# Two-layer hybrid mixing block: matmuls of a set recorded as one scheduled piece, and the first loads and small chains in another order

## The chip, the cores and the metric

The kernel runs on one core of one Trainium2 chip. The metric is the device time of one execution in microseconds (us); lower is better. The core has a matrix engine (TensorE, PE in the profile, with its weight loads as PEld), a vector engine (VectorE, DVE), an activation engine (ScalarE, ACT), a general engine (GpSimd, POOL) and SyncE (SP), which issues the loads and stores here. Matmuls write to the accumulation memory PSUM; all other tiles lie in the on-chip memory SBUF.

## The reference

Two layers of a block on 512 latent tokens and 256 context tokens of width 1024, all in fp32. Each layer makes six modulation vectors from the condition, mixes the tokens in four parallel groups, and ends with a squared-ReLU MLP:

```python
for layer in range(DEPTH):                      # DEPTH = 2
    sh1, sc1, g1, sh2, sc2, g2 = adaln(c, w_mod[layer], b_mod[layer])
    y_ctx, y_lat = mixing_sublayer(modulate(cx, csh1, csc1), modulate(x, sh1, sc1), ...)
    x = x + g1 * y_lat
    x = x + g2 * sq_relu_mlp(modulate(x, sh2, sc2), mlp_w1[layer], mlp_w2[layer])
    # the context cx likewise, in the first layer only
return rms_norm(x, final_g)
```

`adaln` is `silu(cond) @ w + b`, cut into six rows; `modulate` is `rms_norm(x) * (1 + scale) + shift`. `mixing_sublayer` projects the tokens by `w_in` (1024 x 2464) and splits the columns into a gated depthwise convolution of 31 taps, a latent attention (MLA), a grouped attention (GQA), and a chunked retention in two directions whose decay comes from `ret_decay`; the four results go through `w_out`.

## The kernel before

The kernel is written as a list of operations that are recorded, not issued. Each call on `V`, `S`, `G`, `T` or `D` (DVE, ACT, POOL, PE, and SP for loads) goes to `Plan.record`, which notes the operation with its inputs, outputs, an estimated duration and a priority, the place in the recording plus `plan.lag`. `Plan.schedule` then places all operations by a list scheduler: at every moment each engine takes the ready operation of the lowest priority that has room for its tiles. Some operations may go to DVE, ACT or POOL (`VS`, `VG`, `VSG`), and the planner picks the engine. Only then is everything issued, in that order; each engine runs its instructions in order. As all calls go through `issue`, they carry one line number in the profile, L646 before and L662 after.

Large matmuls are made from three fp32r products (`mm3`: high x low, high x high, low x high) with up to 512 columns. Other matmuls run in fp32; each is then two records in the trace. Three kinds of these fill only a part of the array's 128 columns and are meant to lie beside each other:

- `mod_rows` (line 792), a block of a modulation row: 4 matmuls of 32 columns each, one for every 128 rows of a half of the inner dimension, with 256 or 512 output columns. Their left side is `sf`, the silu of the condition.
- `Duo.finish` (line 1070), the output of an attention for a pair of heads: 12 matmuls (4 for context tokens) of 64 columns, two heads in turn, 256 output columns.
- The output of the retention (`s_ret`, line 1434): full-width matmuls with the states and then matmuls of 64 columns for two heads in turn, 128 or 256 output columns.

Before, each of these matmuls was an operation of its own to the planner, with a price for 64 columns or fewer that assumes the neighbour.

The order in which the parts are recorded is written out in the table `ORDER`, one string per layer: `um`, `ug` and `ur` are parts of the input projection, `mla`, `gqa`, `a`, `taps`, `gates`, `ln`, `rin`, `ret`, `read` steps of the four groups, `u` a step of an attention unit, and `todo:n` the n-th later modulation block of layer 0.

At the start the kernel loads the condition (`crow`), makes `sf`, then records the rotary tables `r64` and `r32`, the chain that makes the logarithm of the retention decay (`lgam` from `lz`, some 25 tiny DVE steps and two ACT steps), then the first modulation blocks (`mods(0)`, as `XO` is 0), and for the context pair (tokens 4 and 5) and the two pairs of x: load, sum of squares on ACT, reciprocal root on POOL, scaling, transposes, copies (`xt`, `norm_T`). After that `begin(q)` modulates a quarter of the inner dimension and `um` multiplies it by its quarter of `w_in`, four times (`late`).

## Time and profile before

| what | value |
|---|---|
| median of three runs | 1684.92 us (1681.69 to 1686.33) |
| the profiled execution | 1679.99 us |
| its span, first to last instruction | 1678.3 us |
| PE busy | 1630.6 us, 97% of the span |
| DVE busy | 1234.1 us, 74% |
| ACT busy | 569.9 us, 34% |
| POOL busy | 256.0 us, 15% |
| mean load rate | 98 GB/s |

Busy time is the time in which at least one instruction of the engine runs; matmuls are pipelined, so a busy PE is not a PE at its peak. What a run of matmuls costs is read from the start of its first to the start of what stands behind it. A wait is put down to the engine or load that ended last.

### The profile page before, as it was taken

How to read it: one execution, taken by the hardware profiler on the slowest of the kernel's cores; microseconds unless marked ns; L12 is line 12 of the kernel's file. 1: busy time of each engine (PE TensorE's matmuls, PEld its weight loads, DVE VectorE, ACT ScalarE, POOL GpSimd, SP SyncE). 2: the span in 40 equal slices, each digit the busy share in tenths (PEclk: the TensorE clock that was granted, in tenths of full speed). 3: DMA queues.
4: the chain of work that ended last, by engine and by line, in shares of the span. 5: the costliest groups of instructions: out<-in, count | busy, mean ns of one | idle time of the engine just before them, and what ended most of it. 6: DMA issues, size and time to landing. Idle time of an engine off the chain costs nothing. (4 is left out here: it accounts for less than half of the span.)

```text
span 1678.3 us, 22457 instructions
## 1 busy us (share of the span) xinstructions
PE 1630.6 (97%) x8603; PEld 1337.5 (80%) x8603; DVE 1234.1 (74%) x2093; ACT 569.9 (34%) x1008; POOL 256.0 (15%) x274
## 2 busy tenths in 40 slices
PE   6999999979999999999999999999989999999997
PEld 4888875657888888888888889788768888888886
DVE  5669956686876978767765667698888766666665
ACT  4431555474351111211211126345472512212212
POOL 2121102143010000010000013303032100000001
PEclk9999999999999999999999999999999999999999
DMA  8412126332322443534421212111125232333331
GB/s 298 135 51 58 51 79 181 102 114 88 98 79 88 127 141 96 164 112 126 151 63 51 74 51 86 46 53 33 53 76 169 83 101 91 98 100 94 95 100 51
DMA packets 138906, 164.03 MB, mean 98 GB/s; under 512 B 7466, under 2 KB 94106, under 8 KB 138800
## 3 DMA queue, kind: packets, MB, share of 16 engines
q1 hardware_dynamic: 138800, 162.61, 31.7%
q8 instruction: 67, 1.10, 0.3%
q14 instruction: 39, 0.32, 0.1%
HBM read 156.56 MB, written 2.10 MB: 95 GB/s over the span
## 5 line engine op out<-in xcount | busy, mean ns | idle before, releaser
L646 PE MATMUL b<-m,m 128*128 128x512 f32 (+5 forms) x6468 | 1316.5, 368 | 8.5 <-DVE m L646 5.8
L646 PEld LDWEIGHTS b<-m,m 128*128 128x128 f32 (+1 forms) x6468 | 1083.1, 185 | 221.8 <-DVE m L646 10.9
L646 DVE TENSOR_TENSOR m<-m,m 128x512 f32<-128x512 f32 (+5 forms) x510 | 457.8, 913 | 69.9 <-PE b L646 56.2
L646 ACT CAST m<-m 128x1024 fp32r<-128x1024 f32 (+3 forms) x219 | 197.4, 916 | 616.7 <-PE b L646 443.7
L646 DVE TENSOR_TENSOR m<-b,m 128x512 f32<-128x512 f32 (+9 forms) x309 | 183.1, 606 | 134.9 <-PE b L646 115.6
L646 POOL TENSOR_TENSOR m<-m,m 128x1024 fp32r<-128x1024 f32 (+5 forms) x67 | 130.3, 1949 | 821.0 <-ACT m L646 449.9
L646 PE MATMUL pp<-m,m 128*128 128x512 f32 (+8 forms) x876 | 180.7, 350 | 3.6 <-ACT m L646 1.9
L646 PEld LDWEIGHTS pp<-m,m 128*128 128x128 f32 (+2 forms) x876 | 134.1, 182 | 37.5 <-issue 11.4
L646 DVE TENSOR_TENSOR m<-m 128x512 f32<-128x512 f32 (+1 forms) x100 | 59.2, 592 | 95.1 <-ACT m L646 94.8
L646 PE MATMUL b<-ident,m 128*128 128x128 f32 (+3 forms) x740 | 109.1, 283 | 12.6 <-DVE m L646 9.1
L646 PEld LDWEIGHTS b<-ident,m 128*128 128x128 f32 (+3 forms) x740 | 86.5, 143 | 35.5 <-DVE m L646 12.1
L646 ACT ACTIVATE m<-b 128x512 f32<-128x512 f32 (+1 forms) x115 | 60.9, 532 | 140.6 <-PE b L646 136.3
L646 DVE SCALAR_TENSOR_TENSOR m<-m,sf,m 128x1024 f32<-128x1024 f32 x80 | 101.8, 1284 | 7.5 <-DMA m<-in_w_mod_dram 7.4
L646 DVE SCALAR_TENSOR_TENSOR m<-m,cvw,m 128x783 f32<-128x783 f32 (+1 forms) x120 | 102.0, 896 | 0.4
L646 ACT COPY m<-b 128x512 f32<-128x512 f32 (+4 forms) x109 | 57.2, 542 | 112.3 <-PE b L646 110.3
L646 DVE TENSOR_REDUCE ty<-pp 128x1 f32<-128x768 f32 (+1 forms) x70 | 62.9, 906 | 12.1 <-PE pp L646 10.8
L646 ACT ACTIVATE m<-pp,ty 128x768 f32<-128x768 f32 (+1 forms) x70 | 60.4, 865 | 31.4 <-DVE ty L646 22.1
L646 DVE CAST m<-m 128x512 fp32r<-128x512 f32 (+4 forms) x126 | 58.9, 471 | 7.5 <-PE b L646 2.6
L646 POOL TENSOR_TENSOR ty<-ty,mhalf 128x1 f32<-128x1 f32 (+4 forms) x47 | 56.3, 1202 | 3.1
L646 ACT ACTIVATE m<-m 128x1024 f32<-128x1024 f32 (+4 forms) x65 | 42.3, 654 | 38.0 <-DVE m L646 37.5
L646 DVE TENSOR_SCALAR m<-m,ty 128x512 f32<-128x512 f32 (+3 forms) x94 | 45.0, 512 | 11.6 <-POOL ty L646 10.9
L646 POOL TENSOR_SCALAR ty<-ty 128x2 f32<-128x2 f32 (+4 forms) x43 | 12.6, 292 | 229.4 <-ACT m L646 163.6
(109 smaller groups left out, 620.8 us busy)
## 6 DMA issues: line engine op xcount, KB each, us to landing
m<-in_mlp_w_dram SPq DMA_DIRECT2D x128, 512.0 KB
m<-in_w_mod_dram SPq DMA_DIRECT2D x96, 512.0 KB
m<-in_w_in_dram SPq DMA_DIRECT2D x32, 512.0 KB
m<-in_w_out_dram SPq DMA_DIRECT2D x16, 512.0 KB
m<-in_x_dram SPq DMA_DIRECT2D x8, 512.0 KB
m<-in_w_in_dram SPq DMA_DIRECT2D x8, 416.0 KB
m<-m SPq DMA_DIRECT2D x24, 96.0 KB
m<-in_ctx_dram SPq DMA_DIRECT2D x4, 512.0 KB
```

The costliest lines, as they stand in the source:

```text
L646: op.fn(*[f(a) for a in op.args], **{k: f(a) for k, a in op.kw.items()})
```

## The change

Four edits, and a new table:

- A class `_Tensor` adds `burst`: a list of matmuls is recorded as one operation, whose inputs and outputs are those of all. The planner places it as a whole, and issues its matmuls one behind the other. `mod_rows`, `Duo.finish` and the retention output use it. Its price is 94 ns plus the columns, in proportion to the share of the array.
- The start: the context pair is recorded ahead of the first modulation blocks (`XO = 1`), and the first quarter of the weights of `um` is loaded with them (`w0`). The rotary tables, the decay chain and `own` move from ahead of all this to behind `begin(0)`. A one-element Silu (`warm`) on ACT is recorded ahead of `srow`.
- The convolution's constants of layer 0 (`cdw`, `prm`) get a later priority, 400 places (`PL`).
- `ORDER` has new strings for both layers; all groups keep their steps.

```diff
-XO = 0
+PL = 400
+XO = 1
...
+class _Tensor(_Engine):
+    def burst(self, mms):
+
+        def go(mms):
+            for o, l, r, start, stop in mms:
+                self._r.matmul(self._p.bind(o), lhsT=self._p.bind(l), rhs=self._p.bind(r), start=start, stop=stop)
+
+        return self._p.record(self._n, self._r, go, (), {"mms": mms})
...
+        for o, l, r, _, _ in kw.get("mms", ()):
+            outs.append(o)
+            ins += [l, r]
...
+        if "mms" in kw:
+            return 94 + sum(4 * n(o) / 2.4 * l.ap[-1][1] / 128 for o, l, _, _, _ in kw["mms"])
...
             if ins[0].dtype == F32:
-                if ins[0].ap[-1][1] <= 64:
-                    return 4 * size / 2.4 * ins[0].ap[-1][1] / 128
                 return max(4 * size, 256) / 2.4 + 7
...
+    warm = cst([128, 1], "warm")
+    S.activation(out=warm, in_=mhalf[:, 0:1], func=AF.Silu)
     srow = cst([16, 128], "srow")
...
-            for k in range(4):
-                T.matmul(o[32 * k:32 * k + 32], lhsT=sf[:, k0 + k], rhs=rs[k // nk][:, k % nk], start=k0 == 0, stop=k0 > 0)
+            T.burst([(o[32 * k:32 * k + 32], sf[:, k0 + k], rs[k // nk][:, k % nk], k0 == 0, k0 > 0) for k in range(4)])
...
+        plan.lag = 0 if l else PL
         cdw = smt([31, 256], nm="cdw")
...
+        plan.lag = 0
...
-                ws = [load(0)]
+                ws = list(w0)
...
-                for j in range(n):
-                    for k in range(2):
-                        T.matmul(o[64 * k:64 * k + 64], lhsT=self.vst[k](self.kts[j]), rhs=self.pts[k][j // 2][:, j % 2],
-                                 start=j == 0, stop=j == n - 1)
+                T.burst([(o[64 * k:64 * k + 64], self.vst[k](self.kts[j]), self.pts[k][j // 2][:, j % 2], j == 0, j == n - 1)
+                         for j in range(n) for k in range(2)])
...
         if XO == k:
             mods(0)
+            w0.append(load_w(kview(w_in[0], 512, 928)[:, 0:2], 2, 416))
         xt.update({t: load_x(t) for t in pr})
```

In the retention output the calls of `T.matmul` become entries of a list `mms`, which `T.burst(mms)` records. One of the strings of `ORDER`, the end of layer 0, before and after:

```
"todo:5 taps:4 rin taps:1 u:1 ret u:1 taps ln:1 u:3 ln:1 u:1 read:1 u:2 ln u:3 read:1 u read "
"todo:4 todo:5 u:1 taps:7 rin u:1 ret u:2 taps u:2 ln u:3 read:1 u:2 read:1 u:1 read u "
```

**Where instructions move.** In an order row stand the line, the operation, output and inputs, the output's shape, and how many alike follow each other; `m`, `b` and `pp` are SBUF pages and PSUM banks.

PE in the mixing of layer 0, before: modulation sets (those with `sf`) between transposes and attention scores.

```order
L646 MATMUL b_3212<-m_5571,sf 32x512 x2
L646 MATMUL pp_5391<-ident,m_4637 128x128
L646 MATMUL pp_5390<-ident,m_4699 128x128 x2
L646 MATMUL pp_5390<-ident,m_4800 128x128
L646 MATMUL b_3212<-m_5581,sf 32x512 x2
L646 MATMUL pp_5390<-ident,m_4800 128x128
L646 MATMUL pp_5391<-m_5579,m_5623 128x256 x2
L646 MATMUL b_3213<-m_5579,m_5623 128x256 x2
L646 MATMUL b_3212<-m_5602,sf 32x512
L646 MATMUL pp_5687<-m_5242,m_5512 128x512
L646 MATMUL pp_5687<-m_5218,m_5512 128x512 x2
L646 MATMUL pp_5687<-m_5218,m_5512 128x256 x3
```

After, a place of the same stage:

```order
L662 MATMUL pp_5562<-m_5392,m_5346 128x512
L662 MATMUL pp_5562<-m_5369,m_5346 128x512 x2
L662 MATMUL pp_5562<-m_5369,m_5346 128x256 x3
L83 MATMUL b_3214<-m_5453,sf 32x512 x2
L83 MATMUL b_3214<-m_5508,sf 32x512 x2
L662 MATMUL b_3216<-ident,m_4117 128x128
L662 MATMUL b_3216<-ident,m_5413 128x128
```

The four matmuls of a set, cut into pieces of two or of one before, stand together now, under L83.

PE in the mixing of layer 1, before: the last pieces of an attention set (64x256) whose first matmul stands some 20 rows further up.

```order
L646 MATMUL pp_13590<-ident,m_13573 128x128
L646 MATMUL pp_13590<-ident,m_13596 128x128
L646 MATMUL b_3213<-m_13599,m_12085 64x256
L646 MATMUL pp_13663<-m_13037,m_13319 128x512
L646 MATMUL pp_13663<-m_13319 128x512
L646 MATMUL pp_13663<-m_13153,m_13319 128x256
L646 MATMUL pp_13663<-m_13319 128x256
L646 MATMUL b_3213<-m_13582,m_12085 64x256
L646 MATMUL b_3213<-m_13599,m_12085 64x256
L646 MATMUL b_3213<-m_13582,m_12146 64x256
L646 MATMUL b_3213<-m_13652,m_12146 64x256
```

After, a set of this stage, with the scores of the next unit ahead of it:

```order
L662 MATMUL pp_13334<-m_13181,m_13087 128x512
L662 MATMUL pp_13334<-m_13154,m_13087 128x512 x2
L662 MATMUL pp_13334<-m_13154,m_13087 128x256 x3
L662 MATMUL pp_13351<-m_13181,m_13087 128x512
L662 MATMUL pp_13351<-m_13154,m_13087 128x512 x2
L83 MATMUL b_3216<-m_12357,m_11877 64x256
L83 MATMUL b_3216<-m_13325,m_11877 64x256
```

The set of 12, of which the first two rows are shown, is no longer cut by scores.

ACT at the start, before: `g` is made from the end of the decay chain, and the rows with 128x1024 are the sums of squares of the context and of x.

```order
L646 ACT_TABLE_LOAD
L646 ACTIVATE srow<-crow 16x128
L646 ACTIVATE lz<-lgam 128x16
L646 ACT_TABLE_LOAD
L646 ACTIVATE lz<-lz 128x16
L646 ACTIVATE g_724<-lgc 128x2
L646 ACTIVATE g_2264<-lgc 128x2
L646 ACTIVATE m_3373,ty_3190<-m_3279 128x1024
L646 ACTIVATE m_3383,ty_3190<-m_3282 128x1024
```

After:

```order
L662 ACT_TABLE_LOAD
L662 ACTIVATE warm<-mhalf 128x1
L662 ACTIVATE srow<-crow 16x128
L662 ACTIVATE m_3282,ty_3191<-m_3231 128x1024
L662 ACTIVATE m_3296,ty_3191<-m_3239 128x1024
L662 COPY m_3328<-b_3215 128x512
L662 COPY m_3328<-b_3216 128x512
```

The steps of the decay chain no longer stand ahead of the squares; on SP the two loads of the context stand third and fourth, where they were twelfth and thirteenth.

## Rows read from the trace of the kernel before

**Rows 1.** Page, part 1: engine, busy us, share of the span, instructions.

```profile
PE 1630.6 (97%) x8603; PEld 1337.5 (80%) x8603; DVE 1234.1 (74%) x2093; ACT 569.9 (34%) x1008; POOL 256.0 (15%) x274
```

**Rows 2.** Stretches: length, busy PE PEld DVE ACT POOL, granted clock, load share, GB/s.

```profile
0.00:42.00 42.00, 26.32 (x168) 18.32 (x172) 24.27 (x85) 19.19 (x36) 9.54 (x40) 1.00 0.90 298
...
190.00:400.00 210.00, 199.37 (x1213) 137.48 (x1212) 152.37 (x314) 125.05 (x242) 52.86 (x61) 0.99 0.36 110
400.00:1030.00 630.00, 628.77 (x3234) 538.26 (x3232) 461.03 (x630) 150.01 (x248) 58.05 (x58) 1.00 0.33 101
1030.00:1330.00 300.00, 289.16 (x1708) 238.28 (x1707) 245.88 (x508) 146.62 (x268) 74.26 (x64) 1.00 0.25 73
```

**Rows 3.** Waits of PE, whole span: us in total, times, longest.

```profile
PE b L646 <- DVE m L646: 14.9, 15, 2.9
```

**Rows 4.** Order in time, PE, layer 0: start, us, what, records; modulation pieces.

```profile
270.12 1.05 PE L646 MATMUL b<-m,sf 128*32 128x512 f32 x4
271.10 0.66 PE L646 MATMUL pp<-ident,m 128*128 128x128 f32 x4
...
273.47 1.05 PE L646 MATMUL b<-m,sf 128*32 128x512 f32 x2
274.44 1.32 PE L646 MATMUL pp<-m,m 96*128 96x512 f32 x6
```

**Rows 5.** Order in time, PE, layer 1: an attention set in three pieces.

```profile
1220.86 0.65 PE L646 MATMUL b<-m,m 128*64 128x256 f32 x2
1221.43 0.30 PE L646 MATMUL pp<-ident,m 128*64 128x128 f32 x1
...
1224.56 0.63 PE L646 MATMUL b<-ident,m 128*128 128x128 f32 x4 [0.77 <-DVE m L646]
...
1226.88 0.65 PE L646 MATMUL b<-m,m 128*64 128x256 f32 x2
1227.46 0.50 PE L646 MATMUL pp<-m,m 128*128 128x512 f32 x1
...
1228.35 2.38 PE L646 MATMUL b<-m,m 128*64 128x256 f32 x20
1230.65 1.54 PE L646 MATMUL pp<-m,m 128*128 128x512 f32 x7
```

**Rows 6.** Order in time, PE, first 64 us: four and one of a set.

```profile
34.16 0.64 PE L646 MATMUL b<-m,sf 128*32 128x256 f32 x8
...
54.78 0.62 PE L646 MATMUL b<-m,sf 128*32 128x256 f32 x2
```

**Rows 7.** Order in time, PE, layer 0: an attention set in one piece.

```profile
342.02 2.81 PE L646 MATMUL b<-m,m 128*64 128x256 f32 x24
344.76 1.43 PE L646 MATMUL pp<-m,m 128*128 128x512 f32 x6
```

**Rows 8.** Page, part 5, ACT copies from PSUM: busy, mean ns, idle before.

```profile
L646 ACT COPY m<-b 128x512 f32<-128x512 f32 (+4 forms) x109 | 57.2, 542 | 112.3 <-PE b L646 110.3
```

**Rows 9.** Order in time, ACT, SP and PE, the first 33 us.

```profile
2.88 1.28 ACT L646 ACT_TABLE_LOAD   x1 [2.88 <-DMA crow<-in_c_ctx_dram]
...
15.79 0.30 ACT L646 ACTIVATE g<-lgc 128x2 f32<-128x2 f32 x2 [6.48 <-DVE lgc L646]
15.99 1.04 ACT L646 ACTIVATE m<-m 128x1024 f32<-128x1024 f32 x1
...
20.11 0.40 SPq L646 DMA_DIRECT2D m<-in_w_in_dram  x1
...
19.82 3.85 PE L646 MATMUL b<-ident,m 128*128 128x128 f32 x16 [2.87 <-DVE m L646]
...
29.82 1.86 PE L646 MATMUL b<-ident,m 128*128 128x128 f32 x15
...
32.61 1.22 PE L646 MATMUL pp<-m,m 128*128 128x416 f32 x5
```

More of the change, by code (lines that the diff above doesn't have):

```diff
@@ L123, in __init__ @@
         self.hurry, self.bias = hurry, {"V": bV, "S": bS, "G": bG}
-        self.V, self.S, self.G, self.T, self.D = [_Engine(self, n, e) for n, e in (
-            ("V", nc.vector), ("S", nc.scalar), ("G", nc.gpsimd), ("T", nc.tensor), ("D", nc.sync))]
+        self.V, self.S, self.G, self.D = [_Engine(self, n, e) for n, e in (
+            ("V", nc.vector), ("S", nc.scalar), ("G", nc.gpsimd), ("D", nc.sync))]
+        self.T = _Tensor(self, "T", nc.tensor)
         self.ops, self.tiles = [], {}
@@ L211, in record @@
             k = alt_kw.get(e, kw)
-            op.alts[e] = (getattr(real[e] if isinstance(real, dict) else real, f), self._cost(e, f, outs, ins, k), k)
+            call = f if callable(f) else getattr(real[e] if isinstance(real, dict) else real, f)
+            op.alts[e] = (call, self._cost(e, f, outs, ins, k), k)
         op.port = {e: self._port(e, fn[e] if isinstance(fn, dict) else fn, outs, alt_kw.get(e, kw)) for e in eng}
@@ L1483, in s_ret @@
                         o = psG(nm="oret")
+                        mms = []
                         if seg == 0:
@@ L1486, in s_ret @@
                                 cs = slice(c * 128, (c + 1) * 128)
-                                T.matmul(o[:, cs], lhsT=states[d][c][:, 2 * e:2 * e + 2].rearrange("p h e -> p (h e)"),
-                                         rhs=qdec[d][:, cs], start=c == 0, stop=False)
+                                mms.append((o[:, cs], states[d][c][:, 2 * e:2 * e + 2].rearrange("p h e -> p (h e)"),
+                                            qdec[d][:, cs], c == 0, False))
                         mine = [[x for x in dts if x[0:3] == (d, seg, 2 * e + k)] for k in range(2)]
@@ L1491, in s_ret @@
                             for k, (_, _, h, t, a, b, m) in enumerate(both):
-                                T.matmul(o[64 * k:64 * k + 64, a:b], lhsT=tile_of(ur, t)[:, 256 + h * 64:320 + h * 64], rhs=m,
-                                         start=seg == 1 and i == 0, stop=i == len(mine[0]) - 1)
+                                mms.append((o[64 * k:64 * k + 64, a:b], tile_of(ur, t)[:, 256 + h * 64:320 + h * 64], m,
+                                            seg == 1 and i == 0, i == len(mine[0]) - 1))
+                        T.burst(mms)
                         VS.copy(out=oT[d][e][seg], in_=o[:, 0:(512, 256)[seg]])
@@ L1629, in begin @@
             modulate(0, 0, pr, q, xT[pr, q], xT[pr, q], ht)
-    xt, xT = {}, {}
+    xt, xT, w0 = {}, {}, []
     for k, pr in enumerate(PAIRS):
@@ L1654, in block_kernel @@
     xt = {}
+    r64 = cst([128, 4, 2, 64], "r64")
+    D.dma_start(out=r64, in_=rope64.rearrange("(t p) a d -> p t a d", p=128))
+    r32 = cst([128, 4, 2, 32], "r32")
+    D.dma_start(out=r32, in_=rope32.rearrange("(t p) a d -> p t a d", p=128))
+    lgam = cst([128, DEPTH * 8], "lgam")
+    D.dma_start(out=lgam, in_=ret_decay.rearrange("l d h -> (l d h)").partition_broadcast(128))
+    lz = cst([128, 6, 16], "lz")
+    z0, z1, z2, z3, z4, z5 = [lz[:, i] for i in range(6)]
+    S.activation(out=z0, in_=lgam, func=AF.Abs)
+    S.activation(out=z1, in_=z0, func=AF.Exp, scale=-1.0)
+    V.tensor_scalar(out=z2, in0=z1, scalar1=2.0, scalar2=None, op0=ALU.add)
+    V.reciprocal(out=z3, in_=z2)
+    V.tensor_tensor(out=z2, in0=z1, in1=z3, op=ALU.mult)
+    V.tensor_tensor(out=z3, in0=z2, in1=z2, op=ALU.mult)
+    V.memset(z4, 1.0 / 19.0)
+    for d in (17, 15, 13, 11, 9, 7, 5, 3, 1):
+        V.tensor_tensor(out=z5, in0=z4, in1=z3, op=ALU.mult)
+        V.tensor_scalar(out=z4, in0=z5, scalar1=1.0 / d, scalar2=None, op0=ALU.add)
+    V.tensor_tensor(out=z5, in0=z4, in1=z2, op=ALU.mult)
+    V.tensor_scalar(out=z4, in0=z5, scalar1=-2.0, scalar2=None, op0=ALU.mult)
+    V.tensor_scalar(out=z3, in0=lgam, scalar1=0.0, scalar2=None, op0=ALU.min)
+    V.tensor_tensor(out=lgam, in0=z3, in1=z4, op=ALU.add)
+    lgc = cst([128, DEPTH, 2], "lgc")
+    for h in range(4):
+        hs = slice(32 * h, 32 * h + 32)
+        V.tensor_copy(out=lgc[hs], in_=lgam[hs].rearrange("p (l d h) -> p l d h", l=DEPTH, d=2)[:, :, :, h])
+    own = cst([128, 4], "own")
+    G.memset(own, 0.0)
+    for h in range(4):
+        G.memset(own[32 * h:32 * h + 32, h:h + 1], 1.0)
     yt = ActT(bigt, True)
```

30 lines of the change are left out of this document (removed), and 12 rows, old and new, of the table ORDER.

## The prediction

> **What bounds the kernel now.** I read the engine totals first, then the stages, then who holds up the matrix engine, then the order in time at the places that the change touches. The totals say that TensorE (PE) is busy 1630.6 of 1678.3 us, and VectorE (DVE) 1234.1 [rows 1]. By stage [rows 2]: in 400 to 1030 us (output projection and MLP of layer 0) PE is busy 628.8 of 630, so nothing but fewer or shorter matmuls can shorten it, and the change has none there. Idle time of PE lies in three places: the first 42 us (15.7 idle), the mixing stage of layer 0 (190 to 400 us, 10.6 idle) and that of layer 1 (1030 to 1330 us, 10.8 idle). The longest single entry in what PE waits for is DVE, 14.9 us in 15 waits, none over 2.9 [rows 3]. So two things count: what PE's own instructions cost, and whether DVE, ScalarE (ACT) and the loads keep up.
>
> **Part 1: sets of packed matmuls kept together.** A set is a group of fp32 matmuls that fill only 32 or 64 of the array's columns: 4 of 32 columns by 512 in a modulation row (12 such sets in the mixing of layer 0), 12 of 64 columns by 256 in an attention output (16 large sets and 4 of four). In the trace every one of them is two records, so x4 in a row means two matmuls. The rows show that neighbours of a set run side by side. One modulation matmul alone takes from 273.47 to 274.44, 0.97 us, and two together from 270.12 to 271.10, 0.98 us [rows 4]. With 256 columns, four take 0.64 us and one takes 0.62 [rows 6]. An attention output in one piece takes 342.02 to 344.76, 2.74 us for 12 [rows 7]; the set of [rows 5] was cut by the planner into 1, 1 and 10 matmuls: 0.57, 0.58 and 2.30 us, together 3.45. So a lone 64-column matmul costs as much as a pair, and a lone 32-column one as much as four.
>
> Before, the planner placed each matmul by itself, and the order of PE's instructions shows the pieces. The 12 modulation sets lie in 27 pieces. At 0.98 us each that is 26.5; the pieces that touch another packed piece save some 0.1 us each, so about 25. Whole they are 12 x 0.98 = 11.8. **Saved: 13 us**, all in layer 0. The attention sets lie in 18 pieces of one, 1 of two, 5 of three, 1 of four, 2 of five, 2 of ten, 9 of eleven and 2 of twelve (leaving out those that touch other packed matmuls). From the rows, 12 cost 2.74 and one costs 0.58, so a piece costs 0.15 plus 0.43 for every pair begun: 40 pieces with 113 pairs begun are 54.6 us, and the same 192 matmuls as 16 whole sets 43.7. **Saved: 11 us**, split between the layers. The retention sets (64 columns by 128) are cut in the same way; no row here prices them apart, their whole work is some 72 matmuls of half the length, and I take 2 us, between 0 and 4. Each switch into a packed piece costs PE something as well: the 0.15 us of the formula lies on the way out, and on the way in I allow 0.09; 69 stretches become 38, so 3 us. **Sum of part 1: 13 + 11 + 2 + 3 = 29; I use 28.** It comes from PE's own issue, in stretches in which PE is 95% to 96% busy, so it is on the path unless another engine takes over.
>
> What could take the cover away: by the grouped rows DVE is busy 152 of 210 us in the first stretch and 246 of 300 in the second [rows 2]. If PE needs some 21 us less in the one (all modulation sets, half of the attention sets, 45 of the 69 stretches) and 7 less in the other, DVE stands at 81% and 84%. That is room, but less of it, and chains of small steps have less matmul work to hide behind. Seven of the large subtractions (128x1024) also move from GpSimd (POOL) to DVE over the whole kernel. **I charge 4 us of new idle time**, with bounds of -10 (the new order of steps closes half of the 21 us that are idle now) and +20 (all of the shorter PE time in both mixings turns into waiting). I stand nearer to zero because the largest part of the gain, the modulation sets, lies in layer 0, where DVE has 27% to spare.
>
> The Trainium skill's page TensorEngine Tiling (Array Packing), section Performance Considerations, speaks against the change here: it says that packing speeds up TensorE but not the evacuation of PSUM, and that the copy out may become the bottleneck. By it the gain of part 1 would shrink to what the modulation sets give; the rows with DVE at 73% and 82% do not show that state yet, and the rule is a rival below.
>
> A set that is one step must also wait for its last operand, where single matmuls could start on the first. In the new order 0.9 to 2 us of other matmuls stand between the last transposes and most of the large sets, and the copy between them takes 0.54 us on ACT [rows 8], so I charge nothing; without this cover each set would wait up to 1 us (rival 2). Modulation sets now hold two raw buffers of 512 KB until the set runs, instead of freeing the first early; the idle time of PE in layer 0 is put down to other engines, not to loads, so this is nothing too.
>
> **Part 2: the start.** Before, SP issues the rotary tables, then both modulation blocks (2.1 MB), then the context (1 MB), then x. The context's norm is then held up on ACT: two small activations on the retention constants (g) stand ahead of the squares and end at 16.0, so the squares start at 15.99, and the first transposes of normalised rows run at 19.82; the first large matmul of the input projection runs at 32.61 [rows 9]. SP's row of one-kilobyte loads holds the next weights back to 20.11. After, the context is issued right behind the two condition vectors, the g activations stand behind the norms, and the small loads behind the weights. The context's 1.05 MB at the 298 GB/s of [rows 2] take 3.5 us; the vectors ahead of it are there at 2.88, so it lands at 6.4 at the earliest, and I take 7. Two squares, the power on POOL and the scaling took 3.8 us before (15.99 to 19.82), so the first transposes run at about 11 in place of 19.8. The modulation blocks (2.1 MB) land at about 14; from there to the first large matmul is the tail of PE's sets, two transposes, and five DVE steps, some 6 us: 20 in place of 32.6. But the 32 transposes of x, 0.12 us each (1.86 for 15 at 29.82), were done by 32.6 and are still ahead now: 3.9 us. So 32.6 - 20 - 3.9 = 8.7 at best. Against it: DVE does the norm scalings, modulations and now the retention constants (some 22 steps of 0.2 us) in one line, and the first weights of the second quarter need them all; by that count the second quarter starts 4 to 5 us earlier, not 9. **I take 7 us, bounds 3 to 10.** From there to 190 us PE is busy all the time, so what the start gains stays. The activation that loads the Silu table early saves its 1.3 us off the path, since the first set waits for its weights anyway: nothing. Constants of the convolution that come later are needed only by the taps: nothing.
>
> **Sum.** 1680.0 (the profiled execution: span 1678.3 and 1.7 around it) - 28 - 7 + 4 = 1649. The median of the three runs is 1684.9, 4.9 above the profiled execution, so the median after should be 1649 + 5 = **1654 us**.
>
> **Rivals.**
> 1. DVE and ACT become the bound in both mixings, so that the attention and retention gain (16 us) turns into PE waits while modulation sets and start remain: 1684.9 - 13 - 7 = 1665, and to 1674 if the start gives only 3 and some of the 13 goes too. For it: DVE at 82% in layer 1 and the wait of 0.77 us for it at 1224.56, between two pieces of the cut set [rows 5]. Against: these waits come from chains in single places, not from a full DVE. Chance 0.17.
> 2. Slower: 38 sets in the mixings wait for their last operand with nothing else ready in PE's queue. The gain of 28 + 7 is gone when each waits 0.92 us on average, and 1.1 us gives 1684.9 - 35 + 42 = 1692. For it: PE takes its instructions in order. Against: the matmuls that stand ahead of most sets in the new order. Chance 0.05.
> 3. The rearranged steps also fill half of the idle time in the mixings (10 us) and the start gives its best: 1684.9 - 28 - 10 - 10 = 1637. Chance 0.14.
> 4. The sets stand together but do not run side by side any better, since something between the two records of a matmul parts them: only the start is left, 1684.9 - 7 + 4 = 1682, within 0.3%. Against: [rows 7]. Chance 0.04.
>
> **How the numbers follow.** The forecast has the remaining 0.60, 1654 us with its own bounds of 1646 to 1662. The range reaches into rivals 1 and 3: 1639 to 1671. About 0.3% (5 us) is what a measurement of this kernel can tell from no change. Forecast, rival 1 and rival 3 are faster by more than that: 0.91, of which I leave 0.02 to rival 1's far end; within it 0.06; slower 0.05.
>
> **What would show it.** In the profile after, the rows of packed matmuls in the mixing should read x8 for a modulation set and x24 for an attention set, with 1.0 and 2.74 us to the next start; busy time of the 32-column by 512 group should halve. The first transposes should stand near 11 us, the first large matmul near 20. PE's idle time in the mixings should be near today's 21 us; at 35 or more, rival 1 holds; idle time right ahead of the sets would be rival 2. I am wrong if PE's idle time grows by more than 20 us anywhere or if the start is held by another line of ACT or SP.

## The result and the profile after

The changed kernel takes 1638.72 us (median of 4 runs, 1637.49 to 1640.4) against 1683.87 us for the kernel before in the same comparison: a ratio of 0.9728, interval 0.9707 to 0.9748. The profiled execution after is 1639.49 us with a span of 1636.6; before it was 1679.99 and 1678.3. The forecast was 1654 us with a range from 1639 to 1671, and the measured time lies just below it. The direction held, the size did not: 45 us came off where 31 were forecast.

The engine line of the page after answers [rows 1], and the stretches answer [rows 2]. The stages end earlier now, so the cuts lie at 190, 385, 1010 and 1285 us: start, rest of the input projection, mixing of layer 0, output projection and MLP, mixing of layer 1, remainder. Columns as in [rows 2].

```profile
PE 1596.7 (98%) x8603; PEld 1328.9 (81%) x8603; DVE 1226.8 (75%) x2095; ACT 571.4 (35%) x1015; POOL 232.5 (14%) x266
```

```profile
0.00:42.00 42.00, 27.56 (x195) 19.46 (x195) 26.27 (x87) 18.69 (x35) 9.51 (x40) 0.96 0.97 326
...
190.00:385.00 195.00, 186.42 (x1271) 139.41 (x1270) 159.42 (x324) 117.31 (x237) 49.04 (x62) 1.00 0.39 123
385.00:1010.00 625.00, 624.31 (x3232) 537.25 (x3232) 457.80 (x641) 152.88 (x260) 63.87 (x63) 1.00 0.33 101
1010.00:1285.00 275.00, 267.85 (x1602) 222.93 (x1601) 228.13 (x476) 148.32 (x261) 58.18 (x61) 1.00 0.25 74
```

PE has as many instructions as before (x8603) and is busy 33.9 us less. In the two mixings it is idle 8.6 and 7.2 us (length less busy), where [rows 2] gave 10.6 and 10.8. DVE stands at 82% and 83% there, as forecast (81% and 84%), and yet PE waits less. The waits of PE over the whole span, against [rows 3]:

```profile
PE pp L662 <- DVE m L662: 8.1, 9, 2.6
PE b L83 <- DMA m<-in_w_mod_dram: 7.2, 2, 5.7
PE b L662 <- DVE m L662: 6.2, 12, 1.1
```

The packed sets stand as the change says, and cost what the rows of before priced. Order in time on PE, layer 0 (start, us, what, records, idle before):

```profile
240.56 1.06 PE L83 MATMUL b<-m,sf 128*32 128x512 f32 x8
241.55 0.38 PE L662 MATMUL pp<-m,m 96*128 96x256 f32 x1
241.87 2.81 PE L83 MATMUL b<-m,m 128*64 128x256 f32 x24
244.61 0.66 PE L662 MATMUL b<-ident,m 128*128 128x128 f32 x4
```

A whole modulation set, x8, takes 0.99 us to the next start, and a whole attention set, x24, 2.74, as in [rows 7].

To see where the 41 us lie I summed, over all of PE's matmuls, the time from one's start to the next one's, with idle time taken out and put in a line of its own. "The rest" holds the other matmuls and the time ahead of the first matmul. "Sets, old table" and "sets and start, old table" are experiments below; "sets and table" has the old start.

| us, to the last matmul | before | sets, old table | sets and start, old table | sets and table | after |
|---|---|---|---|---|---|
| packed fp32 matmuls | 109.1 | 83.8 | 82.5 | 82.0 | 81.1 |
| transposes | 117.2 | 117.9 | 115.4 | 110.2 | 108.9 |
| idle between matmuls | 34.3 | 35.6 | 35.2 | 26.1 | 28.1 |
| fp32r matmuls | 1383.5 | 1383.6 | 1386.8 | 1383.7 | 1385.8 |
| the rest | 25.1 | 25.3 | 24.0 | 25.0 | 23.9 |
| sum | 1669.2 | 1646.1 | 1643.8 | 1626.9 | 1627.8 |

The packed matmuls gave the 28 us of the forecast. Beyond that, transposes (8.3) and idle time (6.2) shrank, where the forecast had 4 us of new idle time, and the start is not seen in the last column at all. The columns "sets, old table" and "sets and table" differ by the new strings alone: 9.5 us of idle time and 7.7 in transposes.

### The profile page after: what moved, and what is told of

Same layout as the page of the kernel before. It is cut to its first block, busy times and chain, and to the rows that moved or that the text cites. A ratio compares the mean times of both kernels' runs of the same rounds, so it can differ in the third digit from the quotient of the medians.

```text
span 1636.6 us, 22440 instructions
## 1 busy us (share of the span) xinstructions
PE 1596.7 (98%) x8603; PEld 1328.9 (81%) x8603; DVE 1226.8 (75%) x2095; ACT 571.4 (35%) x1015; POOL 232.5 (14%) x266
## 5 line engine op out<-in xcount | busy, mean ns | idle before, releaser
L662 PE MATMUL b<-m,m 128*128 128x512 f32 (+3 forms) x5998 | 1249.4, 368 | 2.5 <-DVE m L662 1.6
L662 PEld LDWEIGHTS b<-m,m 128*128 128x128 f32 (+1 forms) x5998 | 1044.5, 189 | 192.0 <-DVE m L662 6.6
L662 DVE TENSOR_TENSOR m<-m,m 128x512 f32<-128x512 f32 (+7 forms) x516 | 457.9, 902 | 65.6 <-PE b L662 54.2
L662 ACT CAST m<-m 128x1024 fp32r<-128x1024 f32 (+2 forms) x225 | 202.7, 918 | 623.3 <-PE b L662 429.9
L662 DVE TENSOR_TENSOR m<-b,m 128x512 f32<-128x512 f32 (+8 forms) x318 | 187.0, 600 | 123.9 <-PE b L662 100.8
L662 POOL TENSOR_TENSOR m<-m,m 128x1024 fp32r<-128x1024 f32 (+5 forms) x57 | 107.9, 1901 | 715.9 <-ACT m L662 426.0
L662 PE MATMUL pp<-m,m 128*128 128x512 f32 (+6 forms) x712 | 163.8, 366 | 8.5 <-DVE m L662 6.6
L662 PEld LDWEIGHTS pp<-m,m 128*128 128x128 f32 (+1 forms) x712 | 122.4, 191 | 37.3 <-DVE m L662 8.3
L662 DVE TENSOR_TENSOR m<-m 128x512 f32<-128x512 f32 (+2 forms) x104 | 62.9, 605 | 100.9 <-ACT m L662 100.4
L83 PE MATMUL b<-m,m 128*64 128x256 f32 (+2 forms) x568 | 61.6, 354 | 0.9 <-DVE m L662 0.9
L662 ACT ACTIVATE m<-m 128x1024 f32<-128x1024 f32 (+4 forms) x65 | 42.4, 654 | 40.8 <-DVE m L662 35.2
L662 DVE TENSOR_SCALAR m<-m,ty 128x512 f32<-128x512 f32 (+3 forms) x98 | 45.3, 498 | 14.0 <-POOL ty L662 13.6
```

The lines of the kernel that those rows point to most:

```text
L83: self._r.matmul(self._p.bind(o), lhsT=self._p.bind(l), rhs=self._p.bind(r), start=start, stop=stop)
L662: op.fn(*[f(a) for a in op.args], **{k: f(a) for k, a in op.kw.items()})
```

## Experiments

### One part alone: sets, start, order

Three kernels take the diff apart. The first has the sets, with the old start and the old strings of `ORDER`.

Against the kernel before (the edits of `Duo.finish` and of the retention output as in the diff, too):

```diff
-            for k in range(4):
-                T.matmul(o[32 * k:32 * k + 32], lhsT=sf[:, k0 + k], rhs=rs[k // nk][:, k % nk], start=k0 == 0, stop=k0 > 0)
+            T.burst([(o[32 * k:32 * k + 32], sf[:, k0 + k], rs[k // nk][:, k % nk], k0 == 0, k0 > 0) for k in range(4)])
```

> Only the sets as one step: the start, the priorities and the order table are those of before. Theory (the gain is PE's own issue: 28 us of packed matmuls and their switches): 1684 - 28 = 1656 us, packed stretches in the mixings down from 98.6 us to about 74 as in the changed kernel, idle time of PE in the mixings near the 21 us of before. Rival A (a planner that places whole sets also closes waits, so the new table adds nothing): 1649 or less, with idle time in the mixings near the 17 us of after. Rival B (without the new table the shorter PE work turns into waits): 1665 or more, idle time in the mixings 30 us or more.

Measured: 1655.48 us, ratio 0.9846 (0.9823 to 0.9869). That is 25 to 26 us, and the packed column of the table moves by 25.3. Idle time and transposes grow by 2.0 together. The sets by themselves did what the sum of part 1 says, new idle time included.

The second has the new start, single matmuls and the old strings; against the kernel before:

```diff
-XO = 0
+PL = 400
+XO = 1
...
+    warm = cst([128, 1], "warm")
+    S.activation(out=warm, in_=mhalf[:, 0:1], func=AF.Silu)
...
-                ws = [load(0)]
+                ws = list(w0)
```

> Only the start: context first, first weights with the first modulation blocks, decay chain and constants later, early Silu; single matmuls and the order table of before. Theory (what the start gains stays, because PE is never idle from 40 to 190 us): 1684 - 6 = 1678 us, first transposes of normalised rows near 10 us instead of 19.8, first large matmul near 19.5 instead of 32.6. Rival (given back in the mixing, where the planner's order shifts): 1682 to 1688.

Measured: 1682.05 us, 1.0006 (0.9996 to 1.0017): nothing. Its first large matmul runs at 20.19 us in place of 32.61, so the start moved as forecast; the time did not, as the rival had it. Order in time on PE, start of this kernel, with the idle time ahead in brackets:

```profile
20.19 4.56 PE L664 MATMUL pp<-m,m 128*128 128x416 f32 x12 [2.58 <-DVE m L664]
24.55 2.45 PE L664 MATMUL b<-ident,m 128*128 128x128 f32 x16
27.90 0.63 PE L664 MATMUL pp<-m,m 128*128 128x416 f32 x2 [0.90 <-DVE m L664]
```

Counting the columns that PE has gone through, this kernel is some 3.7 us ahead of the kernel before at 35 us, 1.9 at 42 and 2.1 at 190. It keeps these 2 us until layer 1, where it loses them:

```profile
1136.54 1.90 PE L664 MATMUL pp<-m,m 96*128 96x512 f32 x10 [1.86 <-DVE m L664]
```

```profile
1130.00:1138.00 8.00, 6.14 (x36) 4.99 (x35) 8.00 (x11) 2.87 (x5) 6.49 (x3) 1.00 0.49 145
1138.00:1141.40 3.40, 3.40 (x19) 2.04 (x19) 2.48 (x5) 2.36 (x5) 2.03 (x1) 0.56 0.00 0
```

The first fence is PE's order in time, the second has stretches of the same kernel with the columns of [rows 2]. PE waited 1.86 us for a DVE that was busy all of the 8 us, and then ran at a granted clock of 0.56. No such wait stands there before. The order of the steps had moved a little with the start; the planner goes on from where the start leaves it, but no run shows that this made the wait.

The third has only the new strings of `ORDER`, with single matmuls and the old start; the first line of them:

```diff
-    "um:2 ug:2 um mla:2 ug gqa:2 a:6 gqa mla a ur:4 taps:2 u:1 ur u:1 gates:2 u:1 gates:2 taps:2 gates "
+    "um:4 ug:2 um ug:2 mla:2 ug gqa:1 a:2 gqa:1 a:4 gqa mla a ur:2 u:1 ur taps:2 u:1 gates:2 taps:4 u:1 "
```

> Only the new order table, with single matmuls and the start of before. Theory (the table fits whole sets and is worth little alone): 1684 within 6 us either way, with packed matmuls still cut into some 65 to 75 stretches in the mixings. Rival B (the table is what closes the waits): 1678 or less, idle time in the mixings 15 us or less.

Measured: 1683.06 us, 1.002 (1.0004 to 1.0037). By themselves the new strings are worth nothing, or cost a little.

### Two parts of three

The kernel after, with one part undone each time. Without the new strings:

```diff
-    "um:4 ug:2 um ug:2 mla:2 ug gqa:1 a:2 gqa:1 a:4 gqa mla a ur:2 u:1 ur taps:2 u:1 gates:2 taps:4 u:1 "
...
+    "um:2 ug:2 um mla:2 ug gqa:2 a:6 gqa mla a ur:4 taps:2 u:1 ur u:1 gates:2 u:1 gates:2 taps:2 gates "
```

> The changed kernel with the order table of before: whole sets and the new start. Theory now (the new table is made for whole sets, and closes waits and keeps PE at full clock only with them): ratio to before 0.982 to 0.986, 10 us or more above the changed kernel (0.973), with idle time of PE in the mixings 22 us or more against 17. Rival A (the table adds nothing, sets and start make it all): 0.973 to 0.977.

Measured: 1655.39 us, 0.9844 (0.9812 to 0.9876), 17 us more than the kernel after. So the strings that are worth nothing alone are worth 17 to 19 us beside the sets. Without the new start:

```diff
-PL = 400
-XO = 1
+PL = 0
+XO = 0
...
-    warm = cst([128, 1], "warm")
-    S.activation(out=warm, in_=mhalf[:, 0:1], func=AF.Silu)
```

> The changed kernel with the start of before: whole sets and the new order table. Theory (start worth 6 us, and it stays): ratio 0.976 to 0.978, the first large matmul at 32 us again, everything behind it as in the changed kernel but 6 us later. Rival (as the start alone gave nothing, it gives nothing here either): 0.972 to 0.974. Rival (the rest only works behind the new start): 0.982 or more.

Measured: 1638.08 us, 0.9744 (0.9717 to 0.9771), as fast as the kernel after. Without the sets:

```diff
-            T.burst([(o[32 * k:32 * k + 32], sf[:, k0 + k], rs[k // nk][:, k % nk], k0 == 0, k0 > 0) for k in range(4)])
+            for k in range(4):
+                T.matmul(o[32 * k:32 * k + 32], lhsT=sf[:, k0 + k], rhs=rs[k // nk][:, k % nk], start=k0 == 0, stop=k0 > 0)
```

> The changed kernel with single matmuls: new start and new order table. Theory (packed work is 28 us of it, and the table is worth nothing without the sets): ratio 0.995 to 1.002, packed stretches in the mixings near 100 us. Rival (table and start together are what counts): 0.985 or less.

Measured: 1679.54 us, 0.9986 (0.9972 to 1.0). Start and strings together do next to nothing without the sets. The interaction is shown; why the same strings do not help single matmuls is seen in part. Behind the start this kernel's PE is idle for 8.3 us in layer 0, where the kernel before has 10.6, but for 13.9 in layer 1, where that has 11.4; and between 300 us and the last rows of the kernel it has four stretches of 3.4 us at a granted clock of 0.50, where that has one.

### What the new strings do, layer by layer

The kernel after with the old string in layer 1 (the beginning of the string):

```diff
-    "um mla:1 ug:2 mla:1 ug gqa:1 mla a taps:2 gqa taps:2 u:1 ur:2 u:1 ur u:1 taps:2 gates:2 taps:2 gates "
...
+    "um mla:1 ug:2 mla:1 ug gqa mla a u:1 taps:4 ur:4 u:1 ur u:1 taps:2 gates:2 taps:2 gates taps:2 u:2 "
...
```

> The changed kernel with the new string of the order table for layer 0 alone; layer 1 has the string of before. Theory (each string closes the waits of its own layer, and with them the stretches at half clock; from the traces of the changed kernel and of the one with the old table 9 us in layer 0 and 7 in layer 1): ratio 0.978 to 0.980, no stretch at half clock between 40 and 900 us, one or more in the mixing of layer 1. Rival (one layer's string does nearly all): 0.973 or 0.984.

And with the old string in layer 0 (its end):

```diff
-    "todo:4 todo:5 u:1 taps:7 rin u:1 ret u:2 taps u:2 ln u:3 read:1 u:2 read:1 u:1 read u "
+    "todo:5 taps:4 rin taps:1 u:1 ret u:1 taps ln:1 u:3 ln:1 u:1 read:1 u:2 ln u:3 read:1 u read "
```

> The same with the new string for layer 1 alone, layer 0 as before. Theory: ratio 0.979 to 0.982, stretches at half clock in layer 0 as with the old table, none in the mixing of layer 1. Rival (the two strings only work together): 0.984 or more.

Measured: 1647.61 us, 0.9793 (0.9756 to 0.983), and 1648.76 us, 0.9801 (0.9764 to 0.9837). Each string gives about half, as expected; the stretch at half clock that I expected in layer 1 with the old string did not come. For layer 1 the two kernels can be laid side by side, since both run it at full clock: from 1005 to 1325 us, first the kernel after, then the one with the old string (columns of [rows 2]).

```profile
1005.00:1325.00 320.00, 312.85 (x1828) 261.56 (x1828) 261.09 (x520) 159.87 (x280) 66.11 (x65) 1.00 0.26 79
```

```profile
1005.00:1325.00 320.00, 307.43 (x1805) 255.96 (x1804) 258.95 (x515) 160.12 (x280) 80.23 (x63) 1.00 0.26 76
```

PE is idle 7.2 us with the new string and 12.6 with the old one, so here the string closes 5.4 us of waits. From the layer's first norm to the end of its mixing the new string saves 7.4 us (306.1 against 313.5); the other 2 lie between the starts of transposes, in steps too short to be listed as waits.

In layer 0 the waits are one part, and the clock is another. The kernel without the new strings, in stretches (columns of [rows 2]) and in PE's order in time:

```profile
313.00:320.20 7.20, 4.00 (x30) 3.08 (x30) 7.07 (x18) 6.70 (x11) 1.64 (x4) 1.00 0.00 0
320.20:327.00 6.80, 6.19 (x24) 5.56 (x24) 5.51 (x11) 2.67 (x6) 2.92 (x4) 0.50 0.00 0
```

```profile
320.81 2.93 PE L662 MATMUL b<-m,m 128*128 128x256 f32 x12 [2.41 <-POOL m L662]
...
359.37 1.67 PE L662 MATMUL b<-m,m 128*128 128x256 f32 x12 [0.63 <-DVE m L662]
```

Short waits cluster from 313 us on, PE is busy 4.00 of 7.20 us, the last wait of 2.41 us is for POOL, and for the next 6.8 us the granted clock is 0.50: the 1.2 GHz level. Twelve matmul records of 256 columns take 2.93 us there and 1.67 at full clock at 359. That kernel has two more such stretches, at 350.9 and 1211.1, 3.4 us each. The kernel after has none between 23.4 and 1631 us; the same place in it reads:

```profile
313.00:328.00 15.00, 14.01 (x112) 11.58 (x110) 14.87 (x36) 11.68 (x26) 4.68 (x9) 1.00 0.14 41
```

The 13.6 us at half clock cost at most half of it, 6.8 us, and the whole difference is 16 to 17. So the waits themselves, with the short ones between transposes, are the larger part: waits of 1 us or more behind 42 us sum to 10.7 us without the new strings and to 2.6 in the kernel after. No run was made to part the two, but the executions of the kernel with the sets alone bear on it: 1650.09 us at a mean granted clock of 0.999, 1654.22 at 0.997, 1657.83 at 0.996 and 1656.74 at 0.995. The one whose clock hardly fell is still 12 us above the 1638.08 of the same kernel with the new strings.

### The two kinds of sets

Old start and old strings, and bursts only in `mod_rows`, against the kernel with all sets (the retention output likewise):

```diff
-                T.burst([(o[64 * k:64 * k + 64], self.vst[k](self.kts[j]), self.pts[k][j // 2][:, j % 2], j == 0, j == n - 1)
-                         for j in range(n) for k in range(2)])
+                for j in range(n):
+                    for k in range(2):
+                        T.matmul(o[64 * k:64 * k + 64], lhsT=self.vst[k](self.kts[j]), rhs=self.pts[k][j // 2][:, j % 2],
+                                 start=j == 0, stop=j == n - 1)
```

> Only the modulation matmuls as sets; attention and retention single, start and table of before. Theory (12 sets in place of 27 pieces, 13 us of PE issue, 2 us of switches): ratio 0.990 to 0.993. Rival (as the planner mixes pieces of the two kinds, cutting only one kind gives little): 0.995 or more.

Then bursts only in `Duo.finish` and the retention output:

```diff
-            T.burst([(o[32 * k:32 * k + 32], sf[:, k0 + k], rs[k // nk][:, k % nk], k0 == 0, k0 > 0) for k in range(4)])
+            for k in range(4):
+                T.matmul(o[32 * k:32 * k + 32], lhsT=sf[:, k0 + k], rhs=rs[k // nk][:, k % nk], start=k0 == 0, stop=k0 > 0)
```

> Only the attention and retention matmuls as sets; modulation single, start and table of before. Theory (11 us of attention, 2 of retention, 1 of switches): ratio 0.991 to 0.994, and together with the modulation sets about the 0.985 of all sets. Rival (the attention sets wait for their last operand): 0.997 or more, with PE idle right ahead of sets.

Measured: 1667.1 us, 0.9908 (0.9872 to 0.9945), and 1657.28 us, 0.9847 (0.9803 to 0.9891). The first is near the 13 us of the forecast (its packed matmuls fell by 13.9); the second lies outside what was expected. In the grouped rows of 190 to 400 us the modulation matmuls stand like this, before and with their sets whole:

```profile
L646 PE MATMUL b<-m,sf 128*32 128x512 f32 x64 | 18.7, 604 | 0.0
L646 PE MATMUL pp<-m,sf 128*32 128x512 f32 x32 | 7.2, 604 | 0.0
```

```profile
L83 PE MATMUL b<-m,sf 128*32 128x512 f32 x64 | 8.5, 605 | 0.0
L83 PE MATMUL pp<-m,sf 128*32 128x512 f32 x32 | 4.3, 605 | 0.0
```

25.9 us become 12.8 for the same 96 records. The second kernel is a surprise: the attention sets alone give about as much as all sets, so the two gains do not add. Its order on PE shows the larger part of the reason. The modulation matmuls are still placed one by one, but with no attention matmuls to slip in between they fall together by themselves, in 14 unbroken stretches of two, four and six (before: 22, eight of them of one matmul). To the next start they take 16.4 us in layer 0, where the kernel before has 23.3 and whole sets have 12.0. Order in time on PE:

```profile
225.28 1.91 PE L664 MATMUL b<-m,sf 128*32 128x512 f32 x12
230.84 1.05 PE L664 MATMUL b<-m,sf 128*32 128x512 f32 x4
```

Six matmuls in one stretch keep PE busy for 1.91 us, two for 1.05, and [rows 4] show 1.05 for a lone one as well.

### What makes a set fast: neighbours in different columns

The kernel after, with the matmuls of an attention set ordered by head: all six on one half of the columns, then all six on the other. The set stays one piece.

```diff
-                         for j in range(n) for k in range(2)])
+                         for k in range(2) for j in range(n)])
```

> The changed kernel, but within an attention set first all matmuls of one head (columns 0 to 63), then all of the other (64 to 127); same planner, same order of everything else. Theory (neighbours run side by side only on different columns, and PE's issue sets the time): a set of 12 takes about 12 x 0.43 + 0.15 = 5.3 us instead of 2.74, a set of four 1.9 instead of 1.0: 16 x 2.5 + 4 x 0.9 = 43 us, less the part that fills idle time of PE in the mixings (up to 8): 1674 to 1682 us. Rival (the attention sets lie beside other waits, so the columns do not matter for the end): 1639 to 1655. Rival (adjacency alone is what counts): no change, 1639.

Measured: 1665.95 us, 0.9912 (0.9896 to 0.9929), 27 us more than the kernel after, and less than the 1674 to 1682 of the theory. A set of 12 takes 4.52 us in place of 2.74, not 5.3, and a set of four 1.02, as in the kernel after (1.01), not 1.9:

```profile
243.27 4.59 PE L83 MATMUL b<-m,m 128*64 128x256 f32 x24
247.79 0.66 PE L662 MATMUL b<-ident,m 128*128 128x128 f32 x4
...
254.62 1.09 PE L83 MATMUL b<-m,m 128*64 128x256 f32 x8
255.64 1.32 PE L662 MATMUL pp<-m,m 96*128 96x512 f32 x6
```

16 sets at 1.78 us more are 28.5 us. So it is the side-by-side run of neighbours that pays, and an attention set kept whole without it costs more than the cut one of [rows 5] (3.45 us). Packed matmuls of this kernel sum to 109.6 us, as before the change; its modulation sets still run side by side. The starts of the single records show why 12 take 4.52 us and not 5.3. In the kernel after they stand in 12 pairs, one every 0.21 us: two matmuls run side by side, and each is two records. Ordered by half, they stand one by one, 0.22 us apart, except for four pairs in the middle of the set, where the last two matmuls of one half run beside the first two of the other; these start ahead of matmuls that stand before them in the instructions. In a set of four that is the whole set, so the order does not matter there.

### Where the start's gain goes

The kernel after with rotary tables, decay chain and `own` recorded ahead again:

```diff
+    r64 = cst([128, 4, 2, 64], "r64")
+    D.dma_start(out=r64, in_=rope64.rearrange("(t p) a d -> p t a d", p=128))
...
     srow = cst([16, 128], "srow")
```

> The changed kernel with the rotary tables, the decay chain and own recorded ahead of the context again, all else new. Theory (in the start, the two activations at the end of the decay chain hold up the squares on ACT, as before at 15.79): the context's squares wait for the chain, first transposes 2 to 4 us later than 10.3, and 2 to 4 us more in the end: ratio 0.974 to 0.976. Rival (loads order alone makes the start): first transposes at 10 to 11 us, 0.973.

Measured: 1640.31 us, 0.9755 (0.973 to 0.978). Its first transposes of normalised rows stand at 14.08 us instead of 10.28, as the theory has it, and its first large matmul runs at 23.26 instead of 19.42; the whole is the same within the interval, so the time cannot tell theory and rival apart.

In the kernel after, DVE is busy 9.33 of the 10 us from 30 to 40, with 26 of the decay chain's 30 small steps among them. The next kernel gives that chain a later priority, 400 places, and with it the steps stand at 54 to 72 us.

```diff
+    plan.lag = PL
     lgam = cst([128, DEPTH * 8], "lgam")
...
+    plan.lag = 0
     yt = ActT(bigt, True)
```

> The kernel after, with the decay chain (some 28 small steps on VectorE, 0.17 us each, which stand between 28 and 40 us in its trace) put later, behind the modulation of the first four quarters. Theory: VectorE, busy 9.33 of the 10 us from 30 to 40, is what takes the start's lead away; then PE's idle time in the first 42 us falls by 1 to 2 us against the kernel after and the whole by 1 to 3 us, ratio to the kernel before 0.971 to 0.973. Rival: the loads set the pace of the start (16 DMA engines about full from 10 to 37 us in both kernels); then the order of VectorE's steps gives nothing, the wait of 1.02 us at 38 us stays in another form, and the time is that of the kernel after within 1 us.

Beside it ran the kernel after itself, unchanged, and the kernel without the new start from above.

> The kernel after, beside the two others of this call on one chip, so that 1 to 3 us can be told apart: ratio to the kernel before 0.972 to 0.974 by every theory.

> Sets and new table without the new start, beside the kernel after on one chip. My prediction's term for the start says 7 us more than the kernel after (ratio higher by 0.004); the count of columns done in the two traces says that PE is ahead by 5 us at 20 us, by 1.3 at 50 us, by 0.5 from 100 to 280 us and behind by 1 after that, so this theory expects the same time within 2 us (ratio within 0.0012 of the kernel after).

Measured side by side: 1638.93 us, 0.9738 (0.9709 to 0.9767) with the late chain; 1639.17 us, 0.974 (0.9711 to 0.9768) for the kernel after; 1638.41 us, 0.9736 (0.9707 to 0.9764) without the new start. The start is worth nothing to within some 2 us. From 30 to 40 us, the kernel after and the one with the late chain (columns of [rows 2]), and then PE in the latter:

```profile
30.00:40.00 10.00, 8.98 (x67) 6.10 (x66) 9.33 (x41) 3.06 (x6) 0.00 (x0) 1.00 1.09 353
```

```profile
30.00:40.00 10.00, 8.99 (x66) 6.03 (x65) 7.27 (x17) 2.27 (x5) 0.00 (x0) 1.00 1.09 352
```

```profile
37.64 0.84 PE L662 MATMUL pp<-m,m 128*128 128x416 f32 x3 [1.01 <-DVE m L662]
```

DVE loses 2 us of work and PE still waits 1.01 us at 37.64, where the kernel after waits 1.02 at 38.00. So the length of DVE's line is not what held PE: my theory for this run fell, and the numbers are the rival's. The rival's cause, the loads, is not seen either. The DMA engines are full (share 1.09), but behind 9.27 us no wait of PE in the start is for a load, and DVE, in the kernel with the late chain, waits for PE:

```profile
33.64 0.42 DVE L662 TENSOR_TENSOR m<-b,m 128x256 f32<-128x256 f32 x1 [2.29 <-PE b L83]
33.99 0.58 DVE L662 CAST m<-m 128x832 fp32r<-128x832 f32 x1
34.97 0.18 DVE L662 TENSOR_REDUCE modc<-b 128x4 f32<-128x16 f32 x1 [0.40 <-PE b L662]
35.06 1.02 DVE L662 TENSOR_TENSOR m<-m,m 128x832 fp32r<-128x832 f32 x1
35.99 0.17 DVE L662 TENSOR_SCALAR modc<-modc 128x4 f32<-128x4 f32 x1
36.19 1.06 DVE L662 TENSOR_SCALAR m<-m,modc 128x256 f32<-128x256 f32 x3
37.17 0.76 DVE L662 CAST m<-m 128x512 fp32r<-128x512 f32 x2
```

That is one chain: a modulation set on PE, an addition on DVE (33.64), two transposes on PE, then on DVE the reduction (34.97), an addition of one (35.99), the scaling of the tokens (36.19) and their cast (37.17), and the large matmul at 37.64. It runs 4 us from the set's end. Between its steps on DVE stands the split of a quarter of the weights, the rows of 128x832: the cast fits into the wait for the transposes, the subtraction of 1.02 us stands between the reduction and the next step. So the wait is the length of this chain, with that subtraction in it, as these rows have it; no run shortened the chain or moved the split.

## Why the prediction was too high

**The sets (28 us): right.** Packed matmuls fell by 28.0 us. The modulation term (13) came out as 13 in the run with these sets alone and 12 in the kernel after, and the attention set at 2.74 us as priced. From 190 us on, the 64-column matmuls of 256 columns, nearly all of them the attentions', take 13.7 us less (11, and a part of the 3 for switches), and those of 128 columns, the retention's, 1.9 (2). What I missed is that the two kinds of sets do not add where either stands alone; with both whole the sum still holds.

**New idle time (+4 us): this step failed.** I took the stages as they stood, with shorter PE work in them, and left the rearranged strings of `ORDER` at a bound of -10 and a rival of 0.14. For the sets under the old strings the sign was right: idle time and transposes grew by 2 us. The new strings then took 17 to 19 us off. After the sets (28) and a start worth nothing, the profiled executions (40.5 us apart) leave -12.5 where I wrote +4. Of it, 6.2 us are waits and 8.3 lie in transposes (some 2 go the other way); nearly 4 of the 8.3 lie in the first 42 us, so the pair of kernels that differ by the strings alone, with 9.5 and 7.7, says it more cleanly. The transposes count both short waits and the stretches at half clock that the old strings bring beside the sets and the new ones do not. Rival 3's mechanism, rearranged steps that close waits, is the one that came. That its 1637 us lies so near the measured time is luck: 10 of the 20 us that it adds to the sets were to come from the start, which gave nothing, and a larger gain from the order and the step to the median, below, stand in their place.

**The start (7 us): over-sized.** Each place forecast was met: first transposes of normalised rows at 10.28 (11 forecast), first large matmul at 19.42 (20). In the kernel after:

```profile
9.27 1.08 PE L83 MATMUL b<-m,sf 128*32 128x256 f32 x8 [5.72 <-DMA m<-in_w_mod_dram]
10.28 2.82 PE L662 MATMUL b<-ident,m 128*128 128x128 f32 x12
...
19.42 4.37 PE L662 MATMUL pp<-m,m 128*128 128x416 f32 x12 [2.59 <-DVE m L662]
23.63 1.91 PE L662 MATMUL b<-ident,m 128*128 128x128 f32 x16
...
38.00 0.65 PE L662 MATMUL pp<-m,m 128*128 128x416 f32 x2 [1.02 <-DVE m L662]
```

But the first modulation set stands at 9.27 us in both kernels (9.30 before, behind the same kind of load), and behind it the kernel before was idle little. Its waits there, besides the 2.87 us of [rows 9] and two of 0.24 and 0.47:

```profile
10.71 1.08 PE L646 MATMUL b<-m,sf 128*32 128x256 f32 x8 [0.33 <-DMA m<-in_w_mod_dram]
12.80 0.69 PE L646 MATMUL b<-ident,m 128*128 128x128 f32 x2 [1.01 <-DVE m L646]
...
16.26 0.69 PE L646 MATMUL b<-ident,m 128*128 128x128 f32 x2 [0.91 <-DVE m L646]
...
24.42 4.01 PE L646 MATMUL b<-ident,m 128*128 128x128 f32 x17 [0.75 <-ACT m L646]
```

Together that is 6.6 us, and the kernel after still waits 5.4 there (2.59, 1.02, 0.95, and 0.8 in two small ones), and its granted clock is half from 20.0 to 23.4 us, behind the wait of 2.59, so that 12 large matmuls take 4.2 us to the next start. Against the kernel without the new start, PE is ahead by 5 us of work at 20 us, by 1.3 at 50 and by 0.5 from 100 to 280. The step that failed is the difference of two positions (32.6 less 20, less the transposes of x): it took for idle what the kernel before had filled with transposes and sets. From 24.42 to 32.61, 8.2 us, that kernel does the transposes of x and two sets, where I took off 3.9: 17 transposes take 4.01 us there, 0.24 each, and not the 0.12 of 29.82 [rows 9]. 12.6 less 8.2 are 4.4, near the 5 us of lead at 20 us; the two waits of about 1 us and the stretch at half clock take most of that back by 50. A check was at hand in [rows 2]: 15.7 us idle in 42, of which 9 lie ahead of the first modulation set. It is no bound, since the slow transposes are counted as busy; why they are slow at a granted clock of 1.00 no run shows.

**A set waits for its last operand: nothing was charged, and one case came.** In layer 0 the last modulation set stops in its middle, with everything behind it, until its second weight block has landed:

```profile
288.94 1.05 PE L83 MATMUL b<-m,sf 128*32 128x512 f32 x4
291.48 1.05 PE L83 MATMUL b<-m,sf 128*32 128x512 f32 x4 [1.49 <-DMA m<-in_w_mod_dram]
```

This is rival 2's mechanism, once in this trace, at 1.49 us, and at 0.47 in the second trace of the same kernel; all other modulation sets behind 190 us take their 1.0 us, and all sets of 12 their 2.7. In the kernel without the new start no wait is listed there, but the set takes longer as well:

```profile
289.38 1.85 PE L83 MATMUL b<-m,sf 128*32 128x512 f32 x8
291.17 0.66 PE L662 MATMUL pp<-ident,m 128*128 128x128 f32 x4
```

That is 1.79 us to the next start in place of 0.99. It is here, in this pair of traces, that the last 0.5 us of the start's lead turn into some 1.2 us behind; a single pair does not show that the new start makes the wait longer.

**Rival 1, DVE as the bound: did not come.** The Trainium skill's rule on the copies out of PSUM (TensorEngine Tiling (Array Packing), Performance Considerations) would have taken the attention gain back. This case's traces do not show that state: with the attention sets alone, the 64-column matmuls of 256 columns behind 190 us take 13.4 us less, about as in the kernel after (13.7), with DVE busy 165.1 of the 210 us from 190 to 400.

**The step to the median.** I added 4.9 us, since the three runs of before lay that far above their profiled execution. The profile after lies 0.8 above its median. The lists of executions show what the 4.9 us go with: those of the kernel before whose clock is listed take 1676.8 to 1682.3 us at a mean granted clock of 0.998, where the profiled one lies too, and 1687.7 to 1688.0 at 0.992; the kernel after stays at 0.996 to 0.998 and within 3 us. So the step was not a constant to be carried over. 5 to 6 us of the 15 that the forecast missed by are this step (its 4.9 and the 0.8); the rest is the 16 of the idle term less the 7 of the start.

## What to carry to other kernels

Price a set of packed matmuls by its pieces: a lone narrow matmul costs what its full-width group costs, and the gain is real only where neighbours use different columns. When a change makes pieces larger and also writes a new order for them, the order is a term of its own: here it was worth nothing alone, 17 us with the pieces, by closing waits, the largest of 1 to 2.5 us, and the stretches at half clock behind them. An earlier first step of a start is no gain where other work already filled the time: count what the start must do until the work goes on as before, not where its first step stands.

## What the runs showed of the hardware

- Of the 64-column fp32 matmuls of 256 columns, two in different column halves run side by side, a pair of records every 0.21 us; in the same half their records start one by one, 0.22 us apart. At a change of half, two matmuls of each half overlap: 12 ordered by half take 4.52 us (2.74 in turn), where twelve times 0.43 are 5.2, and four ordered by half 1.02 (1.01 in turn).
- A few waits in a row, 3.2 us idle of 7.2 with none over 2.41, were followed by 6.8 us at the 1.2 GHz level; in the kernel after, whose waits behind the start are at most 1.49 us, no such stretch lies between 23.4 and 1631 us.
- At the start of the kernel before, transposes of 128x128 take 0.24 us each (17 in 4.01 us at 24.42) and 0.12 from 29.82 on (15 in 1.86), with a granted clock of 1.00 over the first 42 us: this column alone does not tell PE's pace there.
